# A planned kernel's tiles: slots given by the plan, the one vacant longest, and taken out of turn

## The chip, the cores and the metric

The kernel runs on one core of a Trainium2 chip. The metric is the device time of one execution in microseconds, the median of several runs; lower is better. The core has five engines that run side by side and wait for each other by semaphores: TensorE (PE in the profile; PEld is its weight load), VectorE (DVE), ScalarE (ACT), GpSimd (POOL) and SyncE (SP), which here issues every DMA. Tiles live in SBUF; TensorE writes its results into PSUM, which has eight banks of 512 fp32 columns for each of 128 partitions.

## The reference

One inference step of a trunk of two layers, for 512 latent tokens and 128 context tokens, with 1024 channels. A layer is RMSNorm, a modulation from the condition (shift, scale, gate), one input projection, three branches that read it, an output projection and a gated residual. Cut to its core:

```python
h = rmsnorm(x, g_norm[l]) * (1 + scale) + shift
(cq, ckv, krope, z_a, dq, dk, dv, z_b, mq, mk, mv, mo, z_c, mg) = split(h @ W_in[l])
# A: latent attention, 4 heads of 128+64, low-rank q (384) and kv (256), shared rotary key
o_a = attention(q_a, [k_a, k_ctx], [v_a, v_ctx], MLA_SCALE)
# B: differential attention, 4 heads, two softmax maps of 64 each
o_b = rmsnorm(attention(q1, k1, v) - lam * attention(q2, k2, v))
# C: bidirectional mLSTM, 4 heads, one scan for each direction
o_c = rmsnorm(sigmoid(mo) * (mlstm(forward) + mlstm(backward)))
y = concat(o_a * silu(z_a), o_b * silu(z_b), o_c * silu(z_c)) @ W_out[l]
x = x + gate * y
```

After two layers comes a last RMSNorm. Latent tokens attend to all 512 latent and 128 cached context keys; context tokens only to themselves. The results are both token streams and the new caches of the context tokens.

## The kernel before

All 640 tokens go through together as five tiles of 128. Products that need more than fp32r holds are made of three fp32r products (`mm3`): each operand is split into a high part (a ScalarE copy to fp32r) and a low part (a subtraction on VectorE or GpSimd).

The kernel doesn't issue an instruction while it is described. `V`, `A`, `G`, `T` and `SP` are recorders, and the object `Plan` keeps every operation with its program order. `Feed` mixes two streams into that order: the branch heads (`mlstm_head`, `diff_head`, `mla_head`) yield the time that they leave to TensorE, and units of projections (in the order of the string `ORDER`) are pulled in to fill it. At the end `issue` does three things: `link` finds which operation depends on which, `simulate` plays a list schedule with estimated durations (`cost`) and delays between engines (`delay`), and the operations are issued in the order of their planned starts. Each engine then works through its queue in that order; on the chip an instruction waits for its semaphores, and what is behind it on its engine waits too.

Tiles have tags with a number of places each (`CAPS`). In SBUF, `qt` gives tiles of 645 columns of the tag `Q`; the slot itself is given by the tile framework when the operations are issued. In PSUM, `pj` and `sm` take one bank of 4 to 7 and `S` a pair out of 0 to 3; the plan chooses the bank:

```python
CAPS = {"pj": 3, "sm": 3, "S": 2, "Q": 35}
BANKS = {"pj": ((4,), (5,), (6,), (7,)), "sm": ((7,), (6,), (5,), (4,)), "S": ((0, 1), (2, 3))}
...
if rank[x] != nxt[tag] or live[tag] >= self.CAPS[tag]:
    return False
...
bank[x] = next(b for b in self.BANKS[tag] if vacant.issuperset(b))
```

`rank` numbers the tiles of a tag in program order, `nxt` is the number whose turn it is. Among the operations of an engine that are ready and whose tiles may be taken, `simulate` takes the one that is first in program order; up to 60 are looked through. In the plan, a place comes free at the moment at which the last operation on its tile ends. VectorE and GpSimd share a port in the plan: an operation with the mark `port` starts only when no other has it. `cost` returns that mark last.

Three stretches are spoken of below. `out_proj` (a branch's output projection; `opc`, `opb`, `opa`) works in two halves of 512 columns: two `gate` tiles are loaded, then for each of five token tiles `xp` is loaded, twelve matmuls go into one `pj` tile, VectorE multiplies by `gate` into `ytmp`, GpSimd adds into `xp`, and a DMA stores it to `xd`. `mla_prep` makes the normalised `cqh`/`cql` (fp32r) and, by `q_stack`, the four `qs` tiles (fp32r), while `opb` still reads the eight tiles `oTh`/`oTl` of branch B. `mla_v` makes the values of branch A in `pj` tiles, copied into `vva`. `out_tail` is the last output projection of a layer; behind it, tile by tile, come the norm and the transposes of `xs` for the next layer. Shorter names: `Pa` and `P` are exponentials of scores, `sz` the gate paths, `wm` weights of the modulation, `xjk` a scratch tile of the norm.

Of the kernel before, what the change touches and what calls it, by code (L numbers as in the profile page):

```python
# [9 lines left out]
F32 = mybir.dt.float32  # L10
# [111 lines left out]
class Plan:  # L122


    CAPS = {"pj": 3, "sm": 3, "S": 2, "Q": 35}
    BANKS = {"pj": ((4,), (5,), (6,), (7,)), "sm": ((7,), (6,), (5,), (4,)), "S": ((0, 1), (2, 3))}

# [85 lines left out]
    def cost(self, o):  # L213


        m, e, k = o["m"], o["eng"], o["k"]
        if m == "dma_start":
            out = o["outs"][0]
            return 430, 0, 4 * self.free(out) * int(out.shape[0]), False
        if e == "PE":  # L220
            if m == "transpose":
                return 109, 273, 0, False
            n = self.free(k["rhs"])
            if "float32r" in str(k["rhs"].dtype):
                return max(111, 0.4535 * n + 3), 175 + 0.4535 * n, 0, False
            return 2 * max(111, 0.845 * n), 280 + max(0, 0.845 * n * 2 - 110), 0, False
        if not o["outs"]:
            return 60, 60, 0, False
        n = max(self.free(x) for x in o["outs"] + o["ins"])
        ptr = any(self.is_ap(x) and self.free(x) == 1 and n > 2 for x in list(o["a"][1:]) + [k.get("scale"), k.get("bias")])  # L230
        psum = any("PSUM" in str(x.space) for x in o["ins"])
        if e == "ACT":
            t = 155 + 0.85 * n + (100 if ptr else 0) + (193 if "accum_out" in k else 0)
            if any("Ln" in str(x) for x in o["a"]):
                return t + 2500, t + 1300, 0, False
            return t - 95, t, 0, False
        wide = sum(self.free(x) > 1 for x in o["ins"]) > 1
        if e == "DVE":
            t = 145 + 1.06 * n
            if m == "tensor_copy" and not psum or m == "memset":  # L240
                t = 145 + 0.53 * n
            elif m == "tensor_tensor_scan":
                t = 145 + 2.08 * n
            elif ptr:
                t += 62
            return t - 80, t, 0, not psum and (wide or m == "tensor_copy" and n > 4)
        if "pow" in str(k.get("op")):
            t = 400 + 155 * n
        elif m == "memset":
            t = 145 + 0.75 * n  # L250
        else:
            t = 165 + 2.2 * n
        return t - 40, t, 0, wide

    def delay(self, a, b):

        return 55 if b == "PE" else 78 if b == "POOL" else 90 if (a, b) == ("DVE", "ACT") else 36

# [52 lines left out]

    def simulate(self, prio, strict=None):

# [16 lines left out]
        uses, nxt, live = {}, {t: 0 for t in self.CAPS}, {t: 0 for t in self.CAPS}  # L330
        vacant, bank = set(range(8)), {}
        for o in ops:
# [4 lines left out]
        for i in range(n) if strict is None else strict:  # L337
            for x in sorted(ops[i]["tiles"]):
                if x not in rank:
                    rank[x] = of[self.tags[x][0]]  # L340
                    of[self.tags[x][0]] += 1
        have = set()
        ready = {e: [] for e in ("PE", "DVE", "ACT", "POOL", "SP")}
# [8 lines left out]
        def may(o):  # L352
            for x in o["tiles"]:
                if x not in have:
                    tag = self.tags[x][0]
                    if rank[x] != nxt[tag] or live[tag] >= self.CAPS[tag]:
                        return False
                    if tag in self.BANKS and not any(vacant.issuperset(b) for b in self.BANKS[tag]):
                        return False
            return True  # L360
        while done < n:
            moved = True
            while moved:
                moved = False
                for e in ready:
# [19 lines left out]
                    for x in o["tiles"]:  # L385
                        if x not in have:
                            tag = self.tags[x][0]
                            have.add(x)
                            nxt[tag] += 1
                            live[tag] += 1  # L390
                            if tag in self.BANKS:
                                bank[x] = next(b for b in self.BANKS[tag] if vacant.issuperset(b))
                                vacant.difference_update(bank[x])
                    start[i] = t
# [17 lines left out]
                    end = max(end, fin)  # L412
                    heappush(ev, (fin, 1, i, ()))
                    heappush(ev, (free[e], 0, -1, ()))
# [16 lines left out]
            while True:  # L431
                t, kind, i, l = heappop(ev)
                if kind == 1:
                    done += 1
                    for x in ops[i]["tiles"]:
                        uses[x] -= 1
                        if not uses[x]:
                            tag = self.tags[x][0]
                            live[tag] -= 1
                            vacant.update(bank.get(x, ()))  # L440
                for s in l:
# [3 lines left out]
                if not ev or ev[0][0] > t:  # L445
                    break
        self.bank = bank
        return start, end

    def issue(self, tc):  # L450
# [5 lines left out]
        def place(x):  # L456
            if not self.is_ap(x) or x.tensor.name not in self.bank:
                return x
            w = list(x.tensor.shape)[-1]
            p, c = divmod(int(x.offset), w)  # L460
            n = self.psum.shape[-1]
            return bass.AP(self.psum.tensor, p * n + 512 * self.bank[x.tensor.name][0] + c,
                           [(n if i == 0 else s, m) for i, (s, m) in enumerate(x.ap)])

# [7 lines left out]
def tile_hybrid(ctx: ExitStack, tc: tile.TileContext, I: dict, O: dict):  # L472
# [7 lines left out]
    pp = ctx.enter_context(tc.tile_pool(name="pp", bufs=1, space=PSUM))  # L480
    plan.psum = pp.tile([P, 4096], F32, name="banks")
    dr = ctx.enter_context(tc.tile_pool(name="dr", bufs=1, space=DRAM))

# [40 lines left out]
    def qt(name, dt=F32, n=TOK):  # L524
        return plan.tile("Q", sb.tile([P, 645], dt, tag="Q", bufs=NQ, name=name))[:, 0:n]

# [1190 lines left out]
```

## Time and profile before

| | |
|---|---|
| median of 3 runs | 1385.41 us (1384.88 to 1390.94) |
| the profiled execution | 1385.4 us, span 1383.5 us |
| busy in the span: TensorE, VectorE, ScalarE, GpSimd | 1302.8, 823.5, 633.1, 387.1 us |
| HBM read and written | 131.38 and 23.46 MB, 112 GB/s over the span |

The time of the execution is 1.9 us longer than the span, which runs from the first to the last instruction that the profile shows. All operations are issued from one line of the kernel, L468, so that groups are told apart by their tiles (`out<-in`), not by lines. A bank can't be seen in a row: every PSUM tile is called `banks`, and every tile out of the two fixed buffers `fix` or `fixr`.

### The profile page before, as it was taken

The numbers are of one execution on the slowest core, as the hardware profiler recorded it, in microseconds if no ns is written. First come the engines' busy times: TensorE is split into PE (matmuls) and PEld (weight loads), VectorE is DVE, ScalarE is ACT, GpSimd is POOL, SyncE is SP. The second block draws the span as 40 slices with busy tenths as digits, with TensorE's granted clock in tenths as the row PEclk, the third lists the DMA queues.
The fourth block names the chain that finished last, engine by engine and source line by source line (L and its number), as shares of the span: only waits on it lengthen the run. The fifth ranks groups of instructions, "written<-read, shape, count | busy, mean of one in ns | idle before, by whom it ended". The sixth has DMA issues, their size and how long they took to land.

```text
span 1383.5 us, 23989 instructions
## 1 busy us (share of the span) xinstructions
PE 1302.8 (94%) x9300; PEld 1208.5 (87%) x9300; DVE 823.5 (60%) x1786; ACT 633.1 (46%) x1333; POOL 387.1 (28%) x335
## 2 busy tenths in 40 slices
PE   7999999999999999999879999999999999988985
PEld 3799999979999998789769999998899999868974
DVE  2576756674757556744374876666655536584436
ACT  5444543443554544345365444443344445434533
POOL 0412422333223114401433232233421202260132
PEclk9999999999999999999989999999999999999998
DMA  9433433274242125423651334234522112251154
GB/s 323 138 89 91 120 89 120 76 221 132 87 131 75 49 76 148 149 80 103 203 167 32 104 100 114 86 104 130 179 80 79 41 47 74 75 167 61 32 198 152
DMA packets 164643, 156.41 MB, mean 113 GB/s; under 512 B 14193, under 2 KB 130593, under 8 KB 164529
## 3 DMA queue, kind: packets, MB, share of 16 engines
q1 hardware_dynamic: 164528, 154.87, 36.6%
q8 instruction: 73, 1.20, 0.3%
q14 instruction: 42, 0.34, 0.1%
HBM read 131.38 MB, written 23.46 MB: 112 GB/s over the span
## 4 chain that ended last, share of the span: by engine, by line
PE 58%; DVE 10%; ACT 4%; DMA 4%; issue 2%; POOL 0%; SPq 0%; DVEq 0%; POOLq 0%; ACTq 0%
PE banks L468 58%; DVE fix L468 2%; DVE fixr L468 2%; DMA gate<-grow 2%; DVE ksl L468 1%; DVE ytmp L468 1%; ACT ksh L468 1%; DVE xs L468 1%; DVE qs L468 0%; ACT fixr L468 0%; ACT qs L468 0%; DMA mb<-msc 0%; DMA krr<-in_cache_mla_krope 0%; DMA fix<-in_W_mod 0%; POOL xp L468 0%
## 5 line engine op out<-in xcount | busy, mean ns | idle before, releaser
L468 PE MATMUL banks<-fixr 128*128 128x256 f32 (+6 forms) x5732 | 822.0, 297 | 25.1 <-ACT Pa L468 6.0
L468 PEld LDWEIGHTS banks<-fixr 128*128 128x128 f32 (+1 forms) x5732 | 753.6, 185 | 45.6 <-ACT Pa L468 7.7
L468 POOL TENSOR_TENSOR fixr<-fix,fixr 128x1024 fp32r<-128x1024 f32 (+4 forms) x51 | 120.1, 2355 | 378.3 <-ACT fixr L468 373.4
L468 ACT CAST fixr<-fix 128x1024 fp32r<-128x1024 f32 (+6 forms) x164 | 164.6, 1009 | 99.9 <-PE banks L468 71.6
L468 DVE TENSOR_TENSOR fixr<-fix,fixr 128x1024 fp32r<-128x1024 f32 (+5 forms) x114 | 146.0, 1283 | 62.2 <-ACT fixr L468 61.4
L468 PE MATMUL banks<-fixr,oTh 128*128 128x512 f32 x480 | 156.0, 405 | 6.5 <-DVE ytmp L468 5.8
L468 DVE TENSOR_REDUCE fix<-banks 128x1 f32<-128x640 f32 (+1 forms) x120 | 84.6, 711 | 67.2 <-PE banks L468 66.1
L468 POOL TENSOR_TENSOR xp<-xp,ytmp 128x512 f32<-128x512 f32 x60 | 82.1, 1379 | 111.1 <-DVE ytmp L468 45.2
L468 PEld LDWEIGHTS banks<-fixr,oTh 128*128 128x128 f32 x480 | 86.8, 189 | 25.6 <-DVE ytmp L468 7.7
L468 PE MATMUL banks<-fixr,oTl 128*128 128x512 f32 x240 | 96.2, 405 | 3.7 <-DVE fix L468 2.9
L468 ACT ACTIVATE P<-banks,fix 128x640 f32<-128x640 f32 (+1 forms) x80 | 56.6, 708 | 82.9 <-DVE fix L468 71.8
L468 DVE TENSOR_TENSOR ytmp<-banks,gate 128x512 f32<-128x512 f32 x80 | 54.0, 686 | 50.9 <-PE banks L468 31.7
L468 POOL TENSOR_TENSOR fix<-fix 128x5 f32<-128x5 f32 (+1 forms) x31 | 32.7, 1056 | 143.6 <-DVE fix L468 143.2
L468 POOL TENSOR_TENSOR mb<-mb,fix 128x128 f32<-128x128 f32 x80 | 45.6, 593 | 48.5 <-DMA mb<-msc 32.9
L468 PEld LDWEIGHTS banks<-fixr,oTl 128*128 128x128 f32 x240 | 45.4, 190 | 14.0 <-DVE fix L468 3.4
L468 ACT COPY PT<-banks 128x640 f32<-128x640 f32 (+1 forms) x80 | 48.0, 605 | 17.2 <-PE banks L468 16.6
L468 ACT ACTIVATE fix<-mb,fix 128x128 f32<-128x128 f32 x144 | 48.0, 394 | 16.0 <-DMA mb<-msc 9.1
L468 POOL TENSOR_TENSOR qk<-qk,fix 128x256 f32<-128x256 f32 x32 | 23.5, 734 | 86.7 <-DVE fix L468 76.8
L468 DVE RECIPROCAL fix<-fix 128x2 f32<-128x2 f32 (+1 forms) x120 | 19.4, 162 | 47.0 <-ACT Pa L468 24.0
L468 DVE TENSOR_TENSOR fix<-banks,fix 128x128 f32<-128x128 f32 (+3 forms) x144 | 31.3, 239 | 26.1 <-PE banks L468 25.0
L468 ACT ACTIVATE Pa<-banks,fix 128x640 f32<-128x640 f32 (+1 forms) x40 | 28.3, 709 | 36.8 <-DVE fix L468 33.0
L468 PE MATMUL banks<-vv,PT 128*128 128x128 f32 x320 | 41.5, 277 | 0.9 <-ACT PT L468 0.9
(192 smaller groups left out, 1852.7 us busy)
## 6 DMA issues: line engine op xcount, KB each, us to landing
fix<-in_W_in SPq DMA_DIRECT2D x56, 512.0 KB, 4.4
fix<-in_W_mod SPq DMA_DIRECT2D x35, 512.0 KB, 3.7
fix<-in_W_in SPq DMA_DIRECT2D x64, 256.0 KB, 2.9
xd<-xp SPq DMA_DIRECT2D x60, 256.0 KB, 2.0
xp<-xd SPq DMA_DIRECT2D x50, 256.0 KB, 4.8
fix<-in_W_out SPq DMA_DIRECT2D x24, 512.0 KB, 3.8
gate<-grow SPq DMA_DIRECT2D x32, 256.0 KB, 4.7
wm<-in_W_mod SPq DMA_DIRECT2D x26, 256.0 KB, 6.2
```

Source lines behind the costliest of these rows:

```text
L468: o["f"](*[place(x) for x in o["a"]], **{k: place(x) for k, x in o["k"].items()})
```

## The change

The slots of SBUF now belong to the plan too. Two large tiles, `slots` (20 slots, fp32) and `slotsr` (15 slots, fp32r), take the place of the 35 slots shared before, and each `Q` or `R` tile is mapped to its slot as PSUM tiles are to their bank. For every tag the plan takes the place that has been vacant longest (`vacant` keeps the time at which each came free). A tile may be taken before its turn when the live tiles and those earlier ones that aren't taken yet still leave a place. A place comes free 60 ns later in the plan. The mark `port` goes by the kind of operation (two tensor inputs; a copy; on VectorE a `tensor_scalar` of more than one element) and no longer by how many inputs have more than one element. `SLACK` is 0 and nothing calls `simulate` with `place`: these parts do nothing here.

```diff
--- before.py
+++ after.py
@@ -122,8 +122,11 @@
 class Plan:
 
 
-    CAPS = {"pj": 3, "sm": 3, "S": 2, "Q": 35}
-    BANKS = {"pj": ((4,), (5,), (6,), (7,)), "sm": ((7,), (6,), (5,), (4,)), "S": ((0, 1), (2, 3))}
+    CAPS = {"pj": 3, "sm": 3, "S": 2, "Q": 20, "R": 15}
+    PLACES = {"pj": ((4,), (5,), (6,), (7,)), "sm": ((4,), (5,), (6,), (7,)), "S": ((0, 1), (2, 3)),
+              "Q": tuple((8 + i,) for i in range(20)), "R": tuple((28 + i,) for i in range(15))}
+
+    SLACK = 0
 
     def __init__(self):
         self.ops, self.tags, self.seq, self.prio = [], {}, {}, 0
@@ -234,7 +237,7 @@
             if any("Ln" in str(x) for x in o["a"]):
                 return t + 2500, t + 1300, 0, False
             return t - 95, t, 0, False
-        wide = sum(self.free(x) > 1 for x in o["ins"]) > 1
+        two = m in ("tensor_tensor", "tensor_tensor_scan", "scalar_tensor_tensor")
         if e == "DVE":
             t = 145 + 1.06 * n
             if m == "tensor_copy" and not psum or m == "memset":
@@ -243,18 +246,18 @@
                 t = 145 + 2.08 * n
             elif ptr:
                 t += 62
-            return t - 80, t, 0, not psum and (wide or m == "tensor_copy" and n > 4)
+            return t - 80, t, 0, not psum and (two or m == "tensor_copy" or m == "tensor_scalar" and n > 1)
         if "pow" in str(k.get("op")):
             t = 400 + 155 * n
         elif m == "memset":
             t = 145 + 0.75 * n
         else:
             t = 165 + 2.2 * n
-        return t - 40, t, 0, wide
+        return t - 40, t, 0, two
 
     def delay(self, a, b):
 
-        return 55 if b == "PE" else 78 if b == "POOL" else 90 if (a, b) == ("DVE", "ACT") else 36
+        return 55 + self.SLACK if b == "PE" else 78 if b == "POOL" else 90 if (a, b) == ("DVE", "ACT") else 36
 
 
     def link(self):
@@ -309,7 +312,7 @@
             o["pre"], o["tiles"] = pre, tiles
             o["occ"], o["lat"], o["bytes"], o["port"] = self.cost(o)
 
-    def simulate(self, prio, strict=None):
+    def simulate(self, prio, strict=None, place=None):
 
         from heapq import heappush, heappop
         ops = self.ops
@@ -328,7 +331,7 @@
             for p in pre[i]:
                 succ[p].setdefault(o["eng"], []).append(i)
         uses, nxt, live = {}, {t: 0 for t in self.CAPS}, {t: 0 for t in self.CAPS}
-        vacant, bank = set(range(8)), {}
+        vacant, bank = {i: -1.0 - i for i in range(43)}, place or {}
         for o in ops:
             for x in o["tiles"]:
                 uses[x] = uses.get(x, 0) + 1
@@ -339,7 +342,9 @@
                 if x not in rank:
                     rank[x] = of[self.tags[x][0]]
                     of[self.tags[x][0]] += 1
-        have = set()
+        early = {t: set() for t in self.CAPS}
+        have, queue = set(), {b: list(l) for b, l in self.tenants.items()} if place else {}
+        tenants = {}
         ready = {e: [] for e in ("PE", "DVE", "ACT", "POOL", "SP")}
         free = {e: 0.0 for e in ready}
         ev, start, dma, port, cold = [], [0.0] * n, 0.0, 0.0, 0.0
@@ -353,9 +358,13 @@
             for x in o["tiles"]:
                 if x not in have:
                     tag = self.tags[x][0]
-                    if rank[x] != nxt[tag] or live[tag] >= self.CAPS[tag]:
+                    if place:
+                        if not all(b in vacant and queue[b][0] == x for b in place[x]):
+                            return False
+
+                    elif live[tag] + rank[x] - nxt[tag] - sum(y < rank[x] for y in early[tag]) >= self.CAPS[tag]:
                         return False
-                    if tag in self.BANKS and not any(vacant.issuperset(b) for b in self.BANKS[tag]):
+                    elif not any(all(b in vacant for b in c) for c in self.PLACES[tag]):
                         return False
             return True
         while done < n:
@@ -386,11 +395,20 @@
                         if x not in have:
                             tag = self.tags[x][0]
                             have.add(x)
-                            nxt[tag] += 1
+                            early[tag].add(rank[x])
+                            while nxt[tag] in early[tag]:
+                                early[tag].remove(nxt[tag])
+                                nxt[tag] += 1
                             live[tag] += 1
-                            if tag in self.BANKS:
-                                bank[x] = next(b for b in self.BANKS[tag] if vacant.issuperset(b))
-                                vacant.difference_update(bank[x])
+                            if not place:
+
+                                bank[x] = min((c for c in self.PLACES[tag] if all(b in vacant for b in c)),
+                                              key=lambda c: max(vacant[b] for b in c))
+                            for b in bank[x]:
+                                del vacant[b]
+                                tenants.setdefault(b, []).append(x)
+                                if place:
+                                    queue[b].pop(0)
                     start[i] = t
                     late = 0.0
                     if o["port"]:
@@ -410,7 +428,7 @@
                     else:
                         fin = t + late + slow + o["lat"]
                     end = max(end, fin)
-                    heappush(ev, (fin, 1, i, ()))
+                    heappush(ev, (fin + 60, 1, i, ()))
                     heappush(ev, (free[e], 0, -1, ()))
                     for to, l in succ[i].items():
                         if to == e and (e == "PE" or strict is not None and not o["bytes"]):
@@ -437,14 +455,14 @@
                         if not uses[x]:
                             tag = self.tags[x][0]
                             live[tag] -= 1
-                            vacant.update(bank.get(x, ()))
+                            vacant.update((b, t) for b in bank[x])
                 for s in l:
                     left[s] -= 1
                     if not left[s]:
                         heappush(ready[ops[s]["eng"]], (prio[s], s))
                 if not ev or ev[0][0] > t:
                     break
-        self.bank = bank
+        self.bank, self.tenants = bank, tenants
         return start, end
 
     def issue(self, tc):
@@ -458,9 +476,11 @@
                 return x
             w = list(x.tensor.shape)[-1]
             p, c = divmod(int(x.offset), w)
-            n = self.psum.shape[-1]
-            return bass.AP(self.psum.tensor, p * n + 512 * self.bank[x.tensor.name][0] + c,
-                           [(n if i == 0 else s, m) for i, (s, m) in enumerate(x.ap)])
+            b = self.bank[x.tensor.name][0]
+            to, at = (self.psum, 512 * b) if b < 8 else (self.sbuf, w * (b - 8)) if b < 28 else (self.sbufr, w * (b - 28))
+            n = int(to.shape[-1])
+            y = bass.AP(to.tensor, p * n + at + c, [(n if i == 0 else s, m) for i, (s, m) in enumerate(x.ap)])
+            return y if x.dtype == y.dtype else y.bitcast(x.dtype)
 
         with tc.manual_schedule():
             for i in sorted(range(len(self.ops)), key=lambda i: (start[i], i)):
@@ -479,6 +499,8 @@
     sb = ctx.enter_context(tc.tile_pool(name="sb", bufs=1))
     pp = ctx.enter_context(tc.tile_pool(name="pp", bufs=1, space=PSUM))
     plan.psum = pp.tile([P, 4096], F32, name="banks")
+    plan.sbuf = sb.tile([P, 20 * 645], F32, name="slots")
+    plan.sbufr = sb.tile([P, 15 * 645], F32R, name="slotsr")
     dr = ctx.enter_context(tc.tile_pool(name="dr", bufs=1, space=DRAM))
 
 
@@ -522,7 +544,7 @@
     r_e, r_s, r_vp = Ring(NE, 256, fix), Ring(NS, 16, fix), Ring(2, 256, fix)
 
     def qt(name, dt=F32, n=TOK):
-        return plan.tile("Q", sb.tile([P, 645], dt, tag="Q", bufs=NQ, name=name))[:, 0:n]
+        return plan.tile("R" if dt == F32R else "Q", sb.tile([P, 645], dt, tag="Q", bufs=NQ, name=name))[:, 0:n]
 
     def et(name):
         return r_e()
```

## Rows read from the trace of the kernel before

**Rows 1.** The page's first part: busy us, share, instructions.

```profile
PE 1302.8 (94%) x9300; PEld 1208.5 (87%) x9300; DVE 823.5 (60%) x1786; ACT 633.1 (46%) x1333; POOL 387.1 (28%) x335
```

**Rows 2.** Stretches: length, then busy by engine, PEclk, DMA share, GB/s.

```profile
0.00:25.00 25.00, 16.56 (x67) 6.64 (x68) 3.96 (x22) 10.78 (x27) 0.33 (x5) 0.97 0.95 332
25.00:50.00 25.00, 23.03 (x125) 11.94 (x124) 15.05 (x24) 14.64 (x25) 7.66 (x5) 0.97 1.00 305
...
660.00:735.00 75.00, 59.53 (x346) 51.14 (x345) 40.28 (x82) 37.86 (x82) 31.33 (x28) 0.91 0.51 165
...
1200.00:1250.00 50.00, 42.05 (x228) 34.53 (x226) 38.22 (x71) 16.85 (x27) 26.60 (x24) 0.95 0.54 173
...
1372.00:1383.50 11.50, 0.71 (x2) 0.00 (x0) 6.82 (x14) 2.17 (x6) 3.25 (x4) 0.50 0.42 161
```

**Rows 3.** Waits of TensorE: us in total, times, longest.

```profile
PE banks L468 <- DVE ytmp L468: 10.8, 9, 4.2
PE banks L468 <- DVE fix L468: 9.8, 5, 4.3
PE banks L468 <- ACT xs L468: 7.8, 4, 5.8
PE banks L468 <- ACT Pa L468: 6.5, 6, 1.6
PE banks L468 <- DVE sz L468: 4.2, 3, 1.9
...
PE banks L468 <- DVE otmp L468: 2.0, 4, 0.6
```

**Rows 4.** Timeline from 656 us: start, us, what, [idle before, releaser].

```profile
656.20 5.71 SPq L468 DMA_DIRECT2D xd<-xp  x4
...
661.96 0.92 SPq L468 DMA_DIRECT2D gate<-grow  x2
...
667.55 1.88 DVE L468 TENSOR_TENSOR ytmp<-banks,gate 128x512 f32<-128x512 f32 x3 [4.28 <-DMA gate<-grow]
...
668.30 0.75 PE L468 MATMUL banks<-fixr,oTh 128*128 128x512 f32 x1 [2.12 <-DVE ytmp L468]
```

**Rows 5.** Timeline from 1236 us.

```profile
1239.69 0.84 PE L468 MATMUL banks<-fixr 128*128 128x256 f32 x5
...
1242.68 3.33 DVE L468 TENSOR_TENSOR qs<-banks,qs 64x640 fp32r<-64x640 f32 x4
...
1246.79 3.57 PE L468 MATMUL banks<-fixr 128*128 128x256 f32 x15 [4.20 <-DVE ytmp L468]
```

**Rows 6.** Waits of GpSimd and VectorE for loads.

```profile
POOL xp L468 <- DMA xp<-xd: 33.0, 10, 8.1
...
DVE ytmp L468 <- DMA gate<-grow: 18.9, 6, 4.6
```

**Rows 7.** VectorE's groups by shape: busy us, mean ns, idle before.

```profile
L468 DVE TENSOR_SCALAR fix<-fix 128x1 f32<-128x1 f32 x134 | 19.7, 150 | 2.4
...
L468 DVE SCALAR_TENSOR_TENSOR fix<-fix 128x1 f32<-128x1 f32 x40 | 14.9, 372 | 1.0
```

**Rows 8.** Timeline from 1158 us.

```profile
1158.85 2.40 POOL L468 TENSOR_TENSOR fixr<-fix,fixr 128x1024 fp32r<-128x1024 f32 x1 [2.43 <-ACT fixr L468]
1158.86 2.40 DVE L468 SCALAR_TENSOR_TENSOR fix<-fix 128x1 f32<-128x1 f32 x1
...
1163.87 0.77 PE L468 MATMUL banks<-fix,P 128*128 128x128 f32 x5 [1.22 <-ACT P L468]
...
1164.58 0.21 DVE L468 SCALAR_TENSOR_TENSOR fix<-fix 128x1 f32<-128x1 f32 x1
```

**Rows 9.** Timeline from 579 us.

```profile
580.47 2.83 ACT L468 CAST qs<-banks 64x640 fp32r<-64x640 f32 x4 [2.98 <-PE banks L468]
...
583.36 0.39 PE L468 MATMUL banks<-fixr,oTl 128*128 128x512 f32 x1
```

**Rows 10.** Waits of SyncE, the DMA queue's own.

```profile
SPq L468 <- POOL xp L468: 124.2, 50, 13.8
```

## The prediction

> **What bounds the kernel now.** I read the page's shares first: TensorE is busy 1302.8 of 1383.5 us, 94%; VectorE has 60%, ScalarE 46% [rows 1]. Nothing else is near being the limit, and the change neither adds nor removes arithmetic. So it can only act on the 80.7 us in which TensorE is idle, and the next view has to say where they lie. The table by stretches does [rows 2]: 8.4 and 2.0 us in the first two 25 us, where the DMA share is 0.95 and 1.00 (the loads bound it), 15.5 in 660 to 735 (the end of layer 0, where each token tile goes through output projection, norm and transposes before layer 1 can start), 8.0 in 1200 to 1250, and 10.8 in the last 11.5. The rest, 36.0 us, is thinly spread. The beginning, the change of layer and the end are chains of data: no slot or bank shortens them. Say 8.4 + 2.0 + 10.8 = 21.2 us out of reach, and most of the 15.5.
>
> Then the waits of TensorE by what ended them [rows 3]. The names tell two kinds apart. `ytmp`, `sz` and `otmp` are tiles that TensorE never reads: it waits for the VectorE instruction that reads a PSUM bank, so as to write into that bank again. These are bank waits: `ytmp` 10.8 us in 9, `sz` 4.2 in 3, `otmp` 2.0 in 4. `xs` (7.8) is data, the layer change. `Pa` (6.5) and `fix` (9.8) mix both kinds.
>
> **The change part by part.**
>
> *The bank.* Before, a tile of the tag `pj` takes the first vacant of banks 4, 5, 6, 7, and an `sm` tile the first vacant of 7, 6, 5, 4. Where the plan thinks that bank 4 has just come free it gives it out again at once, though another may have stood empty for long. If the reader is later than planned, TensorE stands. The change takes the bank that has been vacant longest, so the plan's error has to exceed that bank's vacancy before it is felt. The nearest rows are the `ytmp` and `sz` waits, 10.8 + 4.2 = 15.0 us, all on `pj` banks. Bounds: 0 (the reader stays as late, and the next tile finds the next bank full) to 15.0. I read two places. At 668.3 TensorE had waited 2.12 us; `gate` was issued at 661.96 behind a store in SP's queue, VectorE stood 4.28 us for it and then did three `ytmp` in a row [rows 4]. A fourth bank would have taken this tile. At 1246.79 TensorE waited 4.20 us, because `ytmp` stood in VectorE's queue behind four subtractions for `qs`, 3.33 us from 1242.68 [rows 5]. A fourth bank helps there by one tile of `mla_v` only, six matmuls of this form; five took 0.84 us at 1239.69, so it is about 1 us of the 4.20. So the gain is whole where one tile is held up and a quarter where the reader is stuck. I take half, 8 us. The Trainium skill (Perfetto Trace Analysis, Optimizing Tensor Performance, Matmuls) says that independent matmul groups should rotate through different banks so that reading one overlaps the next group; by that alone the whole 15.0 would go and the sum would end 7 us lower. Rows 5 are why I don't take it.
>
> *The pairs of banks for scores (`S`).* There are two pairs and two tiles may live, so there is a choice only when both are vacant. Bounds: 0 to 4, half of `Pa` + `otmp` = 6.5 + 2.0 = 8.5 [rows 3]. I take 1.5.
>
> *Out of turn.* Before, no tile may be taken before all tiles of its tag that come earlier in the program. A `gate` or `xp` load so can't be issued before the score tiles in front of it have begun. Now it may, as long as room for those is kept. It shows in VectorE's 18.9 us of waiting for `gate` in 6 waits and GpSimd's 33.0 for `xp` [rows 6]: a load that is issued 5 us earlier ends these. What of it TensorE feels is already in the 8 us above, through `ytmp`; I add nothing. TensorE itself may also begin a later group early: of the 36.0 us spread thinly I take 3, bounds 0 and 9 (a quarter).
>
> *The port and the release.* The plan now counts every two-input VectorE operation on SBUF, and every `tensor_scalar` of more than one element, as shutting GpSimd out and the reverse; before, the 128x1 combination of the softmax sums passed for free. The trace shows that it isn't: 40 of them took 372 ns in the mean, a `tensor_scalar` of the same size 150 [rows 7], and one at 1158.86 took 2.40 us, as long as the GpSimd subtraction that began with it; TensorE then stood 1.22 us for `P` [rows 8]. An undisturbed one took 0.21 at 1164.58, so the 40 lose 14.9 - 40 x 0.21 = 6.5 us on VectorE. Bounds: 0 to 6.5; VectorE is idle 40% of the span, which covers most: I take 1.5. The 60 ns by which a slot or bank comes free later in the plan cost the chip nothing by themselves: no instruction is added.
>
> *The rooms.* 35 shared slots become 20 for fp32 and 15 for fp32r. fp32r: in `mla_prep` eight `oTh`/`oTl` are still held by `opb`, six `cqh`/`cql` are live, and the four `qs` make 18. The first `qs` finds the fifteenth slot, the others need `opb` to end. In layer 0 the `qs` copies run from 580.47 and `opb`'s last matmul begins at 583.36 and lasts 0.39 [rows 9]: 583.75 - 581.2 = 2.5 us of delay, on the way to the first scores. In layer 1 `opb` ends before. I take 2.5, bounds 0 (other work fills it) and 3.3 (the whole stretch). fp32: by the code 21 tiles are asked for before the first norm (ten x tiles, ten `wm`, `xjk`), one over the room; the first `wm` are free again within 12 us, while the loads bound this stretch: nothing. In the output projections beside attention I count 17 to 21 (four `gate`, four `sz`, two to four `vva`, three of scores, two outputs, two to four `xp`/`ytmp`): tight at times; 0.5, with the far bound among the rivals.
>
> Sum: - 8 - 1.5 - 3 - 1.5 + 2.5 + 0.5 = - 11 us on the profiled execution's 1385.4 (span 1383.5 and 1.9 around it), which is the median of the runs shown as well: 1374 us, 0.8% less. Something within 0.5%, 6.9 us, can't be told from no change.
>
> **The rivals.**
>
> *The stalls only move.* The late readers stay late (1246.79), order is no cure, and with the next bank full TensorE stands 1 us later. The gains shrink to the places like 668.3: 2.1 of bank and 1.5 of the port, less 2.5 for the `qs`: 1.1 us, 1384. For it: the biggest single bank wait is of this kind. Against: it is 4.2 of 15.0.
>
> *The slots become too few: slower.* An early load now sits on one of 20 slots, and where all are full a load waits in SP's queue with the weights behind it. SP waited 124.2 us in 50 waits for GpSimd's `xp` alone, 2.5 us each [rows 10]. If the first loads of each of the 14 output passes (six halves and a tail per layer) wait that much longer, that is 35 us of late transfers; of 18.9 us for `gate` 10.8 reached TensorE, 57%, so 20 us: 1385.4 + 20 - 11 = 1394. It is slower as soon as 18 us reach TensorE, that is 31 us of late loads, 13 of the 14 passes. For it: my count touches 20. Against: the room that is kept for tiles in turn, and the slot vacant longest. The Trainium skill (Perfetto Trace Analysis, Optimization Strategy) reads repeated bubbles on the engine that should be saturated as a sign that SBUF or PSUM lacks room for the next tile; by it, cutting 35 to 20 speaks for this rival. In the trace the waits rows 3 name are for banks, not for slots, so I keep it low.
>
> *More comes back.* All 15.0 of bank, 4 of `S`, 9 of early groups, 4 of the port, nothing lost: 1385.4 - 32 = 1353.
>
> **How the numbers follow.** Forecast 0.50 (own range 1364 to 1378), more 0.12, stalls move 0.18, slots too few 0.14; 0.06 stays for a worse order for which no row speaks. Faster 0.50 + 0.12 = 0.62, same 0.18, slower 0.14 + 0.06 = 0.20. The range leaves out half of "more" and those beyond the slots' 1394: 1356 to 1396.
>
> **What would show it.** TensorE's waits for `ytmp` and `sz` fall from 15.0 to about 7 us, and VectorE's for `gate` from 18.9 to under 5. The 128x1 combination's mean falls from 372 towards 210 ns. TensorE's busy sum stays near 1300. In layer 0, `qs` starts after `opb`'s last matmul. I am wrong if SP's waits, or TensorE's for DMA, grow: then the slots are too few. If the bank waits vanish and other waits of TensorE take their place, the stalls only moved.

## The result, and the profile after

The kernel after took 1353.03 us in the median of 4 runs (1349.96 to 1355.33); before, run on the same chip, 1387.1 (1384.88 to 1390.94). The ratio is 0.975, with a 95% interval of 0.9719 to 0.9782: 34 us less, 2.5%. I had forecast 1374 and a range of 1356 to 1396. The direction was right, the size was three times as large, and the time lies below the range.

The profiled execution took 1349.96 us, the fastest of the four, against 1385.41 before. The first part of its page, which answers to [rows 1]:

```profile
span 1348.2 us, 24097 instructions
...
PE 1293.0 (96%) x9300; PEld 1208.7 (90%) x9300; DVE 814.2 (60%) x1786; ACT 631.4 (47%) x1333; POOL 377.5 (28%) x335
```

TensorE's idle time fell from 80.7 to 55.2 us. That is 25.5 of the 35.3 us by which the span is shorter; the other 9.8 are busy time, 1302.8 against 1293.0 for the same 9300 matmuls. A matmul's row is longer than the step to the next one (twelve of 128x512 take 3.04 us below, while one alone has 0.39 in [rows 9]), so a short pause is hidden in busy time. Measured from start to start, against the median step of each form, the pauses between matmuls fell by some 36 us (an estimate; the end behind the last matmul is 2 us longer). To see where, I cut the execution after at the points where TensorE has begun as many matmuls as before at 50, 550, 770, 1200 and 1372 us. The table by stretches, columns as in [rows 2], first the four middle ones of the kernel before, then all of the kernel after:

```profile
50.00:550.00 500.00, 489.36 (x3683) 466.71 (x3683) 315.17 (x675) 237.42 (x493) 142.47 (x120) 1.00 0.35 103
550.00:770.00 220.00, 198.83 (x1301) 181.22 (x1300) 123.46 (x253) 101.93 (x210) 66.28 (x57) 0.97 0.37 118
770.00:1200.00 430.00, 419.82 (x3170) 404.43 (x3168) 262.57 (x595) 195.87 (x423) 113.56 (x101) 1.00 0.32 93
1200.00:1372.00 172.00, 154.54 (x964) 137.57 (x962) 96.48 (x208) 70.34 (x152) 53.50 (x45) 0.98 0.37 124
```

```profile
0.00:48.80 48.80, 39.10 (x193) 18.64 (x194) 18.73 (x47) 25.06 (x50) 6.86 (x12) 0.97 1.00 315
48.80:548.50 499.70, 488.68 (x3686) 466.73 (x3684) 317.39 (x680) 238.21 (x496) 143.39 (x120) 1.00 0.36 104
548.50:754.30 205.80, 194.57 (x1303) 180.25 (x1302) 122.37 (x260) 101.62 (x212) 61.22 (x56) 0.98 0.42 130
754.30:1186.50 432.20, 423.63 (x3172) 409.26 (x3171) 262.57 (x594) 198.30 (x425) 118.86 (x105) 0.99 0.32 94
1186.50:1334.40 147.90, 146.38 (x955) 133.68 (x954) 83.99 (x190) 65.72 (x145) 43.82 (x40) 1.00 0.41 130
1334.40:1348.20 13.80, 0.58 (x3) 0.15 (x1) 9.13 (x18) 2.44 (x8) 3.39 (x5) 0.70 0.40 153
```

The second stretch, 500 us before, is as long as it was; the fourth, 430 before, and the end, 11.5 before, are 2 us longer each. The whole gain lies in the third, 220 before, now 205.8, and in the fifth, 172 before, now 147.9. These are the two places where latent attention runs beside output projections, the first with the change of layer behind it. In both, TensorE is idle less (21.2 and 17.5 us before, 11.2 and 1.5 after) and busy less (by 4.3 and 8.2 us), and the granted clock is higher, 0.98 and 1.00 against 0.97 and 0.98; in the fourth it is lower, 0.99 against 1.00. The clock has two levels, 1.2 and 2.4 GHz, which the profile shows as 0.50 and 1.00; a value between is the mean of a stretch. TensorE is busy 19 us at the lower level before and 15 after; half of that is lost, so the clock gives some 2 us of the 35 (an estimate). (The fifth stretch has nine matmuls fewer than before, since the cuts don't fall on quite the same work.)

The waits of TensorE after; the tiles of SBUF are all called `slots` (fp32) or `slotsr` (fp32r) now, so [rows 3] can't be matched name by name:

```profile
PE banks L488 <- ACT slots L488: 12.9, 12, 3.7
PE banks L488 <- DVE fix L488: 8.9, 9, 4.3
PE banks L488 <- DVE slots L488: 8.9, 9, 1.8
PE banks L488 <- ACT fixr L488: 3.2, 2, 2.8
...
PE banks L488 <- DMA slots<-in_W_mod: 0.7, 1, 0.7
```

The 3.7 us is the data chain at the change of layer. Of loads only 0.7 us is left. Among VectorE's waits there is none for `grow` any more (18.9 us in [rows 6]); among GpSimd's none for `xd` (33.0). Since names don't tell, I matched the PSUM addresses in each kernel's list of instructions to the trace: idle time of TensorE of over 0.15 us counts as a bank wait where the matmul behind it begins within 0.25 us of the end of the last read of the bank that it writes. By that count bank waits fell from 38.9 to 10.3 us. All waits of SyncE together, the sign that I had named for too few slots, went from 1142.7 to 1108.7 us (sums of the view's lines).

Two of the small terms can be read directly. The 128x1 combination, as in [rows 7], and a place like that of [rows 8], in the kernel after:

```profile
L488 DVE SCALAR_TENSOR_TENSOR fix<-fix 128x1 f32<-128x1 f32 x40 | 14.3, 357 | 1.1
```

```profile
1143.53 2.41 POOL L488 TENSOR_TENSOR fixr<-fix,fixr 128x1024 fp32r<-128x1024 f32 x1 [2.39 <-ACT fixr L488]
1143.53 2.42 DVE L488 SCALAR_TENSOR_TENSOR fix<-fix 128x1 f32<-128x1 f32 x1
```

The collision is still there, 2.42 us for an operation of 0.21, though the plan now keeps the two apart. And the `qs` tiles of `mla_prep`, as in [rows 9]:

```profile
574.58 0.69 ACT L488 CAST slotsr<-banks 64x640 fp32r<-64x640 f32 x1 [0.99 <-PE banks L488]
...
577.17 3.04 PE L488 MATMUL banks<-fixr,slotsr 128*128 128x512 f32 x12
577.91 2.12 ACT L488 CAST slotsr<-banks 64x640 fp32r<-64x640 f32 x3 [2.64 <-PE banks L488]
```

The first `qs` takes the fifteenth slot; the copies of the other three stand 2.64 us. They begin 0.7 us into `opb`'s last twelve matmuls, not behind the last of them as I had expected. TensorE works through it.

### The profile page after: what moved, and what is told of

Same layout as the page of the kernel before. It is cut to its first block, busy times and chain, and to the rows that moved or that the text cites. A ratio compares the mean times of both kernels' runs of the same rounds, so it can differ in the third digit from the quotient of the medians.

```text
span 1348.2 us, 24097 instructions
## 1 busy us (share of the span) xinstructions
PE 1293.0 (96%) x9300; PEld 1208.7 (90%) x9300; DVE 814.2 (60%) x1786; ACT 631.4 (47%) x1333; POOL 377.5 (28%) x335
## 4 chain that ended last, share of the span: by engine, by line
PE 79%; DVE 8%; ACT 5%; issue 2%; DMA 1%; POOL 1%; DVEq 0%; SPq 0%; POOLq 0%; ACTq 0%
PE banks L488 79%; DVE slots L488 3%; DVE slotsr L488 2%; ACT slotsr L488 2%; DVE fixr L488 1%; ACT fixr L488 1%; DVE fix L488 1%; ACT slots L488 1%; POOL fixr L488 0%; POOL slots L488 0%; DMA xd<-slots 0%; DMA fix<-in_W_ukv 0%; DMA fix<-in_W_in 0%; DMA slots<-grow 0%; POOL fix L488 0%
## 5 line engine op out<-in xcount | busy, mean ns | idle before, releaser
L488 PE MATMUL banks<-fixr,slotsr 128*128 128x512 f32 (+3 forms) x990 | 236.0, 375 | 0.5 <-ACT slotsr L488 0.3
L488 ACT ACTIVATE slots<-banks,fix 128x128 f32<-128x128 f32 (+3 forms) x250 | 144.0, 582 | 171.7 <-DVE fix L488 94.3
L488 PEld LDWEIGHTS banks<-fixr,slotsr 128*128 128x128 f32 x990 | 170.6, 189 | 26.2 <-ACT slotsr L488 0.8
L488 ACT COPY slots<-banks 128x128 f32<-128x128 f32 (+3 forms) x212 | 85.9, 425 | 131.2 <-PE banks L488 126.8
L488 PE MATMUL banks<-fix,slots 128*128 128x128 f32 x808 | 121.3, 278 | 20.7 <-ACT slots L488 11.2
L488 POOL TENSOR_TENSOR slots<-slots,fix 128x128 f32<-128x128 f32 (+3 forms) x132 | 83.8, 650 | 197.0 <-DVE fix L488 90.0
L488 PEld LDWEIGHTS banks<-fix,slots 128*128 128x128 f32 x808 | 96.5, 144 | 32.2 <-ACT slots L488 13.8
L488 POOL TENSOR_TENSOR slots<-slots 128x512 f32<-128x512 f32 x70 | 86.6, 1240 | 137.7 <-DVE slots L488 104.1
L488 PE MATMUL banks<-slots 128*128 128x128 f32 (+1 forms) x848 | 113.0, 277 | 4.1 <-DVE fix L488 3.1
L488 PEld LDWEIGHTS banks<-slots 128*128 128x128 f32 x848 | 104.0, 191 | 9.6 <-DVE fix L488 4.2
```

Of the source, the lines that this page charges most:

```text
L488: o["f"](*[place(x) for x in o["a"]], **{k: place(x) for k, x in o["k"].items()})
```

## The experiments

Each run stands beside runs of the kernel before on the same chip. "Less" is 1 minus the ratio, times 1386 us. The two parts that were left after reading the profile are the choice of the bank and the turns; all kernels named b_ are the kernel before with parts added, those named a_ the kernel after with parts taken away. The expectations speak of three theories of what made the gain: the bank, the turns, or a truer plan (port marks and the 60 ns). Of each edit the deciding lines are shown; the lines that keep count of vacant places and of tiles taken early are left out.

**The two parts, each undone and each alone.** The bank vacant longest, alone in the kernel before (`b_lru`; undone in `a_first`):

```diff
-bank[x] = next(b for b in self.BANKS[tag] if vacant.issuperset(b))
+bank[x] = min((c for c in self.BANKS[tag] if all(b in vacant for b in c)),
+              key=lambda c: max(vacant[b] for b in c))
```

Out of turn alone (`b_turn`; undone in `a_inturn`):

```diff
-if rank[x] != nxt[tag] or live[tag] >= self.CAPS[tag]:
+if live[tag] + rank[x] - nxt[tag] - sum(y < rank[x] for y in early[tag]) >= self.CAPS[tag]:
```

> The kernel after, but PSUM banks go out as before: the first vacant one (sm from the other end); slots, turns, port and the 60 ns stay. If the choice of the bank made the gain (bank theory), most of the 34 us are lost: 1372 or more, with TensorE's waits for the readers of banks back at 30 us or more. If taking tiles out of turn made it (turn theory), it stays under 1360. If the truer plan made it (plan theory), also under 1360.

> The kernel after, but every tile must wait for its turn as before; banks and slots still go to the place vacant longest. Turn theory: 1372 or more, and VectorE waits again for the gate loads (18.9 us before, none after). Bank theory: 1350 to 1362. Plan theory: 1350 to 1362.

> The kernel before, with one thing alone: a PSUM tile takes the bank vacant longest. Bank theory: 1365 to 1372, TensorE's waits for ytmp and sz (15.0 us) nearly gone. Turn and plan theory: 1378 to 1387, my own forecast for this part alone was 8 + 1.5 us less.

> The kernel before, with one thing alone: a tile may be taken out of turn when there is still room; slots by the framework, banks the first vacant. Turn theory: 1365 to 1372, VectorE's 18.9 us for gate gone. Bank theory: 1380 to 1387, since a bank given out at once after a late reader stalls whatever the order. Plan theory: 1380 to 1387.

| kernel | median us | ratio to before | interval |
|---|---|---|---|
| a_first | 1369.84 | 0.9873 | 0.9856 to 0.989 |
| a_inturn | 1366.48 | 0.9853 | 0.9838 to 0.9867 |
| b_lru | 1377.45 | 0.9939 | 0.9922 to 0.9955 |
| b_turn | 1367.55 | 0.9863 | 0.9843 to 0.9883 |

None of the three theories holds alone. The bank is worth 8.5 us in the kernel before, close to my forecast for that part (8 + 1.5), and 17 in the kernel after; turns are worth 19 and 14. In `b_lru` TensorE waits less for `ytmp` and `sz`, 8.6 us against 15.0 in [rows 3], but more for other VectorE tiles (`oTl` stood at 0.7 before), and VectorE waits for `gate` as long as ever (18.9 in [rows 6]):

```profile
PE banks L470 <- DVE ytmp L470: 6.4, 3, 3.5
...
PE banks L470 <- DVE od L470: 4.0, 4, 1.4
PE banks L470 <- DVE cq L470: 3.9, 2, 3.6
PE banks L470 <- DVE oTl L470: 3.7, 2, 2.9
...
PE banks L470 <- DVE sz L470: 2.2, 2, 1.5
```

```profile
DVE ytmp L470 <- DMA gate<-grow: 21.6, 8, 4.4
```

In `a_inturn` the wait for `gate` is back, and with it TensorE's for VectorE's readers of banks (8.9 in the kernel after), although every tile gets the bank vacant longest:

```profile
PE banks L488 <- DVE slots L488: 20.2, 18, 2.7
```

```profile
DVE slots L488 <- DMA slots<-grow: 13.6, 4, 4.6
```

In `b_turn` no wait for `gate` is left, while bank waits remain or have grown (`sz` was 4.2 in [rows 3]):

```profile
PE banks L472 <- DVE sz L472: 6.5, 4, 2.7
PE banks L472 <- DVE ytmp L472: 5.3, 4, 2.1
```

**Which tiles out of turn, and what the rest is worth.** `b_turn_sb` adds `tag != "Q" and rank[x] != nxt[tag]` as a refusal, so that only SBUF tiles leave their turn; `b_turn_ps` has `tag == "Q"` there. `b_lru_turn` has both edits shown above. `a_port_no60` is the kernel after with the old `wide` marks and `fin` in place of `fin + 60`.

> The kernel before, with SBUF tiles alone allowed out of turn; PSUM tiles keep their turn, banks are the first vacant. If the 19 us of taking tiles out of turn are early loads and early work on VectorE, ScalarE and GpSimd (load theory): 1366 to 1373, no wait for gate left. If they are groups of matmuls that begin early in another bank (group theory): 1380 to 1387.

> The kernel before, with PSUM tiles alone allowed out of turn; SBUF tiles keep their turn. Load theory: 1380 to 1387, VectorE still waits some 19 us for gate. Group theory: 1366 to 1373.

> The kernel before with both parts: the bank vacant longest, and tiles out of turn; port marks, 60 ns and the framework's slots as before. If the two parts add (9.4 and 19.3 us alone): 1355 to 1361, and port, 60 ns and planned slots make up the other 5 us. If they need each other's company to work (each undone cost 14 to 17): below 1355, and those rest parts are worth nothing.

> The kernel after with the old port marks and without the 60 ns. If a truer plan is worth what I forecast: 1.5 us slower, 1353 to 1357; if it carries the other 5 us: 1356 to 1362, with the 128x1 combination on VectorE back near 372 ns in the mean; if it is worth nothing: 1350 to 1355.

| kernel | median us | ratio to before | interval |
|---|---|---|---|
| b_turn_sb | 1360.73 | 0.9812 | 0.9794 to 0.983 |
| b_turn_ps | 1384.02 | 0.9974 | 0.9961 to 0.9987 |
| b_lru_turn | 1350.14 | 0.9729 | 0.9708 to 0.9749 |
| a_port_no60 | 1353.8 | 0.9758 | 0.9737 to 0.9779 |

SBUF turns alone are worth 26 us, more than SBUF and PSUM turns together (19); PSUM turns alone 3.6. `b_lru_turn` already has all of the gain, 37.6 us, which is 10 more than its parts have alone. So the planned slots, the new marks and the 60 ns together add nothing that shows (0.9729 without them, 0.975 with them, the intervals overlap), and `a_port_no60` bears this out for the last two. In `b_turn_ps` the wait for `gate` stays:

```profile
DVE ytmp L472 <- DMA gate<-grow: 14.5, 6, 4.3
```

**Loads or work, and slots.** `b_turn_dma` lets only a load (`o["bytes"]`) take an SBUF tile out of turn, `b_turn_nodma` only the others. `a_slotfirst` is the kernel after with the first vacant slot (`fit[0]`) for `Q` and `R`. `b_lru_turn_sb` joins `b_lru` and `b_turn_sb`.

> The kernel before; out of turn only where the operation that takes the SBUF tile is a load. If the 26 us of SBUF turns come from loads that are issued earlier (load theory): 1360 to 1366, waits for gate gone. If they come from VectorE, ScalarE and GpSimd starting on free tiles early (compute theory): 1378 to 1387.

> The kernel before; out of turn for every operation on SBUF tiles except loads. Load theory: 1380 to 1387, VectorE waits 15 to 20 us for gate as before. Compute theory: 1360 to 1368.

> The kernel before with the bank vacant longest and SBUF tiles alone out of turn. If taking PSUM banks out of turn is harmful in itself (it cost 7 us on top of SBUF turns with first vacant banks): 1343 to 1349, below the kernel after. If it was harmful only by giving out banks just vacated: 1349 to 1354, the same as with both.

> The kernel after, but the SBUF slot given is the first vacant, not the one vacant longest; banks as in after. If the choice of slot matters as that of the bank does (slot theory): 1358 or more, SyncE's waits longer. If slots are rarely reused at once or nobody waits for them: 1350 to 1356.

| kernel | median us | ratio to before | interval |
|---|---|---|---|
| b_turn_dma | 1371.44 | 0.9902 | 0.9883 to 0.9922 |
| b_turn_nodma | 1370.35 | 0.9886 | 0.986 to 0.9912 |
| b_lru_turn_sb | 1344.34 | 0.9716 | 0.9686 to 0.9745 |
| a_slotfirst | 1359.67 | 0.9808 | 0.9781 to 0.9835 |

Both theories were half right: loads alone bring 14 us, other work alone 16, both together 26. `b_turn_dma` has no wait for `gate` left; in `b_turn_nodma`, where I had expected 15 to 20 us of it, there are 7.3 of the 18.9, though no load leaves its turn:

```profile
DVE ytmp L472 <- DMA gate<-grow: 7.3, 4, 4.3
```

So a load is also issued earlier when the work whose turn comes before it is done earlier. It shows again in the tiles `xs`, the tokens' last loads before the change of layer. The same view of the kernel before, of `b_turn_dma`, of `b_turn_nodma` and of `b_turn_sb`, each with count, min/median/max ns and first and last start:

```profile
L468 SPq DMA_DIRECT2D xs<-xd x10: 319/410/438, 687.4 to 708.1; - x10
...
L468 POOL TENSOR_TENSOR xs<-xs,ytmp x5: 1270/1277/1633, 695.2 to 712.7; 128x512 f32<-128x512 f32 x5
```

```profile
L472 SPq DMA_DIRECT2D xs<-xd x10: 320/441/829, 671.4 to 692.3; - x10
...
L472 POOL TENSOR_TENSOR xs<-xs,ytmp x5: 1282/1295/1667, 689.6 to 704.2; 128x512 f32<-128x512 f32 x5
```

```profile
L472 SPq DMA_DIRECT2D xs<-xd x10: 319/396/456, 677.0 to 699.7; - x10
...
L472 POOL TENSOR_TENSOR xs<-xs,ytmp x5: 1265/1284/1299, 687.0 to 704.2; 128x512 f32<-128x512 f32 x5
```

```profile
L472 SPq DMA_DIRECT2D xs<-xd x10: 319/381/667, 664.3 to 686.1; - x10
...
L472 POOL TENSOR_TENSOR xs<-xs,ytmp x5: 1267/1278/1297, 683.9 to 699.3; 128x512 f32<-128x512 f32 x5
```

Before, the first addition comes 7.8 us after the first load, in `b_turn_dma` 18, in `b_turn_nodma` 10, in `b_turn_sb` 20; the last addition begins 8, 8 and 13 us earlier than before. The plan of the kernel before tells the same in its own times: the first load of `xs` has all that it reads at 639.5 us and is planned at 672.6, and in between nothing but its turn holds it.

The choice of slot: `a_slotfirst` came out above the kernel after, 0.9808 against 0.975, each beside its own runs of the kernel before; but the kernel after, run again, is at 0.9763 (`a_slack2`, below) and 0.9777 (`after_again`), and these intervals overlap. VectorE does wait there for stores whose slot is given out again:

```profile
DVE slots L491 <- DMA xd<-slots: 6.1, 4, 2.0
```

In the kernel after that is 0.4 us. TensorE's waits, 42.4 us in all against 41.2, don't show it, so a cost of 4 to 8 us is likely, but not settled.

**The lockstep, the banks' turns, and two controls.** `b_turn_att` lets only the tiles whose names begin with `Pa_` or `PT_` out of turn. `a_inturn_ps` is the kernel after with PSUM tiles in turn. `a_slack2` sets `SLACK = 2`, `a_rel50` has `fin + 50`.

> The kernel before; out of turn only the tiles Pa and PT (scores and their transposes in the latent attention). Lockstep theory (a score tile had to wait until the projection tiles in front of it in the program had begun, and these for their loads): 6 to 12 us less than before, 1373 to 1379. If the 14 us lie elsewhere (output projections, norms): 1382 to 1387.

> The kernel after with PSUM tiles in turn; SBUF tiles out of turn, LRU banks and the rest stay. If banks out of turn cost time in themselves: 1343 to 1349. If they do nothing beyond the schedule's scatter: 1349 to 1357.

> A control: the kernel after with 2 ns more in the plan's delay to TensorE. No cause that I know should move the time; what it differs from 1353 is the scatter of the schedule. I expect at most 4 us.

> A second control: places come free 50 ns later in the plan, not 60. As above: at most 4 us from 1353.

| kernel | median us | ratio to before | interval |
|---|---|---|---|
| b_turn_att | 1375.55 | 0.9929 | 0.9905 to 0.9952 |
| a_inturn_ps | 1348.27 | 0.973 | 0.9706 to 0.9754 |
| a_slack2 | 1351.99 | 0.9763 | 0.974 to 0.9786 |
| a_rel50 | 1353.7 | 0.9776 | 0.9749 to 0.9803 |

Two kinds of tile out of turn, neither of them ever loaded, are worth 10 us, with the wait for `gate` as it was:

```profile
DVE ytmp L472 <- DMA gate<-grow: 16.8, 8, 4.6
```

So most of the part that isn't loads is score tiles held by their turn. What they were held by is only partly what I had in mind. In the plan of the kernel before, operations that begin a `Pa` or `PT` tile in the two latent stretches stand ready for 27.9 us until their turn comes: 15.1 of it behind the `Pa` of the next token tile, 12.8 behind others, mostly `ytmp` of a projection. Which of the two holds brought the 10 us was not tried. `a_slack2` turned out to be no control of the schedule: its list of instructions is that of the kernel after, in order, places and waits, so it is a repeat of it. `a_rel50` differs from the kernel after at 3023 of 8618 places of TensorE's queue, mostly by another slot or bank; another matmul of the program stands at 198. Both stay within 0.3% of the kernel after. So 4 us and less can't be put down to a cause here, and the 5 us of `a_inturn_ps` barely.

**A version that beats both.** The kernel after and `b_lru_turn_sb` again, side by side on one chip:

> The kernel after, unchanged, for a comparison on one chip with best_again: 1350 to 1355.

> The kernel before with the bank vacant longest and SBUF tiles alone out of turn, a second time: 1343 to 1348 if it beats the kernel after by the 5 to 9 us seen; 1349 to 1354 if that was scatter of the runs.

The kernel after took 1353.57 us, 0.9777 (0.9759 to 0.9794) of before; the version 1346.84, 0.9727 (0.9709 to 0.9744). The intervals are apart: the two parts without planned slots, new marks, 60 ns and PSUM turns are 0.5% faster than the whole change. Which of the parts left out cost the time is open: `b_lru_turn`, with PSUM turns, had 0.9729 too.

```profile
span 1341.8 us, 23972 instructions
...
PE 1291.7 (96%) x9300; PEld 1206.8 (90%) x9300; DVE 817.5 (61%) x1786; ACT 632.6 (47%) x1333; POOL 392.6 (29%) x335
```

The lengths of five stretches, cut at the 193rd, 3876th, 5177th and 8347th matmul record of TensorE in each trace (in the kernel before near 50, 550, 770 and 1200 us), in us:

| kernel | start | mLSTM, differential, layer 0 | latent, layer 0 | mLSTM, differential, layer 1 | latent, layer 1, and end |
|---|---|---|---|---|---|
| before | 50.2 | 500.5 | 219.9 | 431.3 | 181.6 |
| b_lru | 52.2 | 497.8 | 216.0 | 427.5 | 182.3 |
| b_turn_dma | 47.9 | 503.4 | 211.3 | 433.8 | 174.1 |
| b_turn_att | 51.0 | 499.8 | 212.2 | 429.6 | 179.4 |
| b_turn_sb | 48.7 | 501.4 | 204.9 | 441.7 | 162.0 |
| b_turn | 48.3 | 508.4 | 204.4 | 444.4 | 163.5 |
| b_lru_turn | 48.4 | 503.2 | 205.1 | 431.5 | 160.9 |
| best_again | 48.3 | 496.9 | 204.4 | 431.3 | 160.9 |

This shows where the parts meet. Turns of SBUF tiles shorten the two latent stretches by 15 and 20 us and lengthen the fourth by 10; turns of PSUM tiles add 7 in the second. The bank vacant longest takes the loss of the fourth back and part of that of the second, which is why it is worth twice as much beside turns as without them. The waits tell why: `ytmp` and `sz` cost TensorE 15.0 us before and 8.6 in `b_lru`, but 11.8 in `b_turn` and 1.3 in `b_lru_turn`.

Much of the lengthening is the clock. The table shows the fourth stretch of `b_turn_sb`, to be compared with 430.00 us, 419.82 of them busy, at 1.00 before. Then come the three times in it at the lower level, and the matmul with which TensorE goes on in the first of them:

```profile
755.00:1196.70 441.70, 427.84 (x3172) 412.78 (x3171) 268.56 (x596) 198.11 (x426) 124.69 (x103) 0.98 0.32 95
947.30:954.10 6.80, 6.15 (x17) 4.98 (x18) 4.46 (x11) 1.66 (x4) 2.50 (x2) 0.50 0.21 80
1015.50:1018.90 3.40, 3.40 (x16) 3.40 (x17) 0.69 (x3) 1.10 (x2) 0.00 (x0) 0.50 0.58 174
1135.00:1141.80 6.80, 6.50 (x31) 6.50 (x31) 5.21 (x12) 2.88 (x7) 2.38 (x1) 0.50 0.24 77
```

```profile
947.62 0.63 PE L472 MATMUL banks<-ksh,qs 128*128 128x320 f32 x1 [2.52 <-DVE ksl L472]
```

So 8.0 of the 11.7 us by which this stretch is longer are busy time, as much as half of the 16.05 that TensorE is busy at 1.2 GHz. In each of the three cases TensorE had just stood for 2.5 to 2.7 us. From `b_turn` to `b_lru_turn`, 19.9 us of span, idle time gives 10.0 and busy time 9.9; TensorE is busy at the lower level for 38.6 us in the one and 19.4 in the other.

## Why the prediction was wrong

*The step that failed is "Out of turn".* It counted early loads at nothing ("What of it TensorE feels is already in the 8 us above, through `ytmp`") and early work at 3 us. Turns measured 19, those of SBUF alone 26: 14 with loads alone, 16 with other work alone, 10 with the score tiles alone. I had priced the part by the waits that bear a load's name. But a tile's turn ties two streams to each other: a load couldn't be issued, and a score tile not be taken, before the tiles in front of it in the program had begun. No row of the profile names that delay; it is already in the order in which the plan issues. TensorE's share of it bears other names: in `b_turn_sb` its waits for `Pa` are gone (6.5 before) and those for `xs` are 4.0 (7.8 before).

Bank and turns together were forecast at 8 + 1.5 + 3 = 12.5 us and measured 37.6 in `b_lru_turn`: 8.5 from the bank, 19 from turns, and 10 that neither has alone and that the sum had no term for.

*"It can only act on the 80.7 us in which TensorE is idle"* was not right either: 9.8 of the 35.3 us came from the busy sum, which I had expected to stay near 1300. By the estimates above most of that is short pauses and little the clock, but the clock has a large part in how bank and turns meet.

*"The beginning, the change of layer and the end are chains of data: no slot or bank shortens them"* was wrong for the change of layer. Its chain starts with ten loads of `xs`, and these waited for their turns; `b_turn_sb` issues them from 664.3, not from 687.4. Over the same matmuls, by count, in which TensorE is idle 15.5 us before (660 to 735 in [rows 2]), it is idle 8.1 us in `b_turn_sb` and 6.9 in the kernel after. For the beginning (10.4 us idle before, 9.7 after) and the end (10.8 and 13.2) it held.

*The bank* was sized well where it stands alone: 8 + 1.5 forecast, 8.5 measured, and the waits for `ytmp` and `sz` fell to 8.6 where I had said about 7. Some luck is in it, since other waits of TensorE grew and its idle time fell by 5.3 us only. What I didn't foresee is that beside turns it is worth 17. That turns hand out more banks that were only just vacated would explain it, but is not shown. With the whole 15.0 of the waits I would still have been short, since they are counted without turns.

*The port and the release*, forecast at 1.5, are worth nothing that can be measured: `a_port_no60` is at 0.9758, within the controls' scatter. The mean of the combination fell from 372 to 357 ns, not towards 210. The two that begin together at 1143.53 are kept apart in the plan, so here the plan's times are not the chip's to within the 0.2 us of such an operation.

*The rooms* cost nothing that shows; in `b_lru_turn`, with the 35 shared slots, the time is the same within the intervals. The delay of the `qs` came, 2.64 us for 2.5 forecast, but TensorE had twelve matmuls to do meanwhile. I had taken it for a delay on the path without naming what else was ready.

*The rivals.* "The slots become too few" fell: TensorE waits 0.7 us for loads (2.2 before), and SyncE's waits did not grow. The Trainium skill's reading of bubbles as lack of room (Perfetto Trace Analysis, Optimization Strategy) doesn't fit the bubbles of the latent stretches: with the same 35 places, `b_turn_sb` takes TensorE's idle time from 21.2 to 11.8 us in the third stretch and from 28.3 to 14.2 in the last, by the order in which places may be taken. "The stalls only move" fell too, by the stretches, though in `b_lru` some did. "More comes back" gave 1353, the time measured, by luck, from another sum: it had 9 us for what turns brought and 4 for a port that brought nothing.

What stays open: why TensorE stalls more in the second and fourth stretch with turns; which of the two holds on score tiles mattered; and whether the slot vacant longest is worth the 4 to 8 us between `a_slotfirst` and the kernel after. Slots were not tried with more or fewer places.

## What to carry to other kernels

When a planner hands out places, ask what its order of handing out ties together: streams in one pool that must take turns run in lockstep, and no wait in the profile bears that name, so price it by the idle time of the stretch in which both run, not by the waits for the late loads. Let a tile go ahead where those before it keep their room, loads above all, and give out the place that has been vacant longest: for banks this cost nothing here and forgave the plan's errors, the more so the freer the order. Look at TensorE's busy time beside its idle time: it hides short pauses, and where the clock falls after a stall, the stall costs more than its own length. Then undo each part of such a change by itself: here planned slots, new marks, the 60 ns and PSUM turns brought nothing together, and leaving them out was faster.

## What I had not expected of the hardware

VectorE's 128x1 operation and GpSimd's 128x1024 subtraction that began in the same nanosecond show 2.42 and 2.41 us, where the first takes 0.21 to 0.22 alone: the time for which it was held appears in its own row, as busy, not as idle before it.

The granted clock goes with the scatter between executions of one kernel. Of the kernel after, 1349.96 us has 0.991 and 1355.33 has 0.985; of `b_turn`, 1365.25 has 0.987 and 1370.76 has 0.982. Between single executions of one kernel, 5 us went with the clock here.
